# Four matmuls of a modulation burst, placed side by side in the columns of TensorE

## The chip, the cores and the metric

The kernel runs on one core of one Trainium2 chip. The metric is the device time of one launch in microseconds (us); lower is better. The program computes in float32 throughout: matrices go through TensorE either as float32 (two passes through the array for one matmul in the code, as the instruction counts show) or as pairs of `float32r` tiles, a rounded part and its remainder.

## The reference, cut to what matters

Two layers of a diffusion backbone over 1024 latent tokens and 256 context tokens, width 1024. Each layer is modulated: a vector of 6144 numbers is computed from the condition `c` (for the latent tokens) and another from `c_ctx` (for the context tokens), and its six parts of 1024 serve as shift, scale and gate.

```python
mod_x = (c_act @ p['w_mod'] + p['b_mod'])[:, None, :]
mod_c = (cctx_act @ p['w_mod'] + p['b_mod'])[None, None, :]
sh1x, sc1x, g1x, sh2x, sc2x, g2x = jnp.split(mod_x, 6, axis=-1)
hx = rms_norm(x, p['g_norm1']) * (1.0 + sc1x) + sh1x
# input projection, differential attention | S5 | Fourier mixing, concatenation
x = x + g1x * (mix_x @ p['w_out'])
x = x + g2x * sq_relu_mlp(rms_norm(x, p['g_norm2']) * (1.0 + sc2x) + sh2x, p)
```

The product for the modulation has two rows only (`c` and `c_ctx`), 1024 terms and 6144 columns, so it reads 25 MB of weights for each layer and uses two columns of the TensorE array.

## The kernel before, in words

The first layer's modulation is computed in two places. `mod_first` (L306) makes the first 16 of its 48 blocks of 128 columns while the inputs load. The other 32 blocks, as eight wide blocks of 512 columns, come from `mod_pe` (L394), a generator that runs as a filler inside the first layer's attention. The second layer's modulation is computed on VectorE, in `mod_rest`, and the change leaves it alone.

For a wide block `mod_pe` needs 1024 terms, that is eight matmuls of 128 terms by 512 columns. It takes them in two bursts of four (`hf` 0 and 1). A burst loads four weight tiles of 128x512 (L403, SP's queue; the tiles of two bursts alternate between two sets of buffers, so the load of a burst waits until the burst before the last has let go of its set). Its four matmuls accumulate in one PSUM bank (L417); the stationary operand is two columns of `cf`, the two activated conditions. ScalarE copies the 2x512 result out (L418). After the second burst eight small transposes (L424) bring both halves into 128 partitions, and `mod_apply` (L291) adds the bias (L295), adds the second half (L297, only when it is given four columns) and, for the two scale parts, forms a factor with the norm's weights.

The attention (`attention`, L618) works through 10 tiles of 128 queries (tiles 8 and 9 are context, with 256 keys instead of 1280) and four heads in each: 40 units. A unit computes scores on TensorE (L649; the context part into a bank called `C`, the rest into the pool `s`), maxima on VectorE (L656, L663), exponentials on ScalarE (L665, L666), a combination on VectorE (L677), transposes on TensorE (L691), copies on ScalarE (L692) and the product with the values on TensorE (L695). The part from L677 on runs three units behind the scores. Banks of PSUM: four for the scores of `s`, and four in the pool `b`, which `C`, the transposes, the product with the values, the bursts and the burst's transposes share. After three units of four the loop calls the filler once: first `glu`, then `mod_pe`, so that each wide block takes three calls: first burst, second burst, transposes. The order of the instructions on each engine is worked out by a planner from the priority of the code's order and from modelled durations; each engine then runs its list in order.

The activated conditions are put into `cf` and `cs` at the start of `mod_first` (L309 to L314), early in the kernel.

Of the kernel before, what the change touches and what calls it, by code (L numbers as in the profile page):

```python
# [19 lines left out]
AX = mybir.AxisListType  # L20
# [14 lines left out]
KD = D // 128  # L35
# [32 lines left out]
class Block:  # L68
# [236 lines left out]
    def mod_first(self, l):  # L305
        nc, io = self.nc, self.io  # L306
        W0 = []
        cs = self.c1([128, KD, 4], 'cs', F32R)
        cf = self.cf = self.c1([128, KD, 4], 'cf')  # L309
        ca = self.cact.rearrange('p v k -> p k v')  # L310
        nc.vector.memset(cf, 0.0)
        nc.vector.tensor_copy(cf[:, :, 0:2], ca)
        nc.scalar.copy(cs[:, :, 0:2], ca)
        nc.vector.tensor_tensor(cs[:, :, 2:4], ca, cs[:, :, 0:2], ALU.subtract)  # L314
        for b in range(2):
            ps = [self.pf((4, 512)) for _ in range(2)]
            for k in range(KD):
                raw = self.s5([128, 1024])
                self.fetched = nc.sync.dma_start(raw, io['w_mod'][l, k * 128:(k + 1) * 128, b * 1024:(b + 1) * 1024])
                if b:  # L320
                    W0 += self.in_weights(l, 3, (k,))
                if k % 2 == 0:
                    for j in range(2):
                        nc.tensor.matmul(ps[j], cf[:, k], raw[:, j * 512:j * 512 + 512], start=(k == 0), stop=(k == KD - 1))
                    continue
                w = [self.tl('rt' if b else 'w4', [128, 1024], F32R) for _ in range(2)]
                self.split(raw, *w)
                for j in range(2):
                    for e in range(2):
                        nc.tensor.matmul(ps[j], cs[:, k], w[e][:, j * 512:j * 512 + 512],  # L330
                                         start=(k == 0 and e == 0), stop=(k == KD - 1 and e == 1))
            pt = self.pb((128, 8, 4))
            for j in range(2):
                o = self.tl('qk', (4, 512))
                (nc.scalar.copy, nc.vector.tensor_copy)[j](o, ps[j])
                for i in range(4):
                    nc.tensor.transpose(pt[:, j * 4 + i], o[:, i * 128:i * 128 + 128], self.idn[0:4, 0:4])
            self.mod_apply(l, b * 8, 8, pt)
        return W0
# [54 lines left out]
    def mod_pe(self, l, blocks):  # L394
        nc, io = self.nc, self.io
        bursts = [(b, hf) for b in blocks for hf in range(2)]

        def load(i):
            b, hf = bursts[i]
            ws = []  # L400
            for q in range(4):
                w = self.tl('t2' if i % 2 else ('r2', 'r2', 'r2', 'mw')[q], [128, 512])
                nc.sync.dma_start(w, io['w_mod'][l, (hf * 4 + q) * 128:(hf * 4 + q + 1) * 128, b * 512:b * 512 + 512])  # L403
                ws.append(w)
            return ws

        nxt = load(0)
        yield
        for i, (b, hf) in enumerate(bursts):
            ws = nxt  # L410
            if i + 1 < len(bursts):
                nxt = load(i + 1)
            if hf == 0:
                o = self.bg((2, 2, 512))
            p = self.pb((2, 512))
            for q in range(4):
                nc.tensor.matmul(p, self.cf[:, hf * 4 + q, 0:2], ws[q], start=(q == 0), stop=(q == 3))  # L417
            nc.scalar.copy(o[:, hf], p)  # L418
            yield
            if hf:  # L420
                pt = self.pb((128, 4, 4))
                for j in range(4):
                    for e in range(2):
                        nc.tensor.transpose(pt[:, j, 2 * e:2 * e + 2], o[:, e, j * 128:j * 128 + 128], self.idn[0:2, 0:2])  # L424
                self.mod_apply(l, b * 4, 4, pt)
                yield

    def norm_rb(self, rs, w):
# [1009 lines left out]
```

## Time and profile before

| | |
|---|---|
| time, median of three runs | 3086.21 us (3080.57 to 3086.28) |
| the profiled execution's own time | 3082.04 us |
| span of the profiled execution | 3080.3 us |
| PE busy | 2948.4 us, 96% of the span |
| DVE (VectorE) busy | 1980.6 us, 64% |
| ACT (ScalarE) busy | 1074.5 us, 35% |
| POOL (GpSimd) busy | 590.7 us, 19% |
| attention of the first layer | about 429 to 730 us of the span |
| the sixteen bursts | 473 to 685 us of the span |

PE is TensorE's matmuls and transposes, PEld its weight loads, DVE is VectorE, ACT ScalarE, SPq the queue that issues DMAs. PEclk is the granted clock as a share of full speed. L417 is line 417 of the kernel. A busy PE in this table is not a full PE: matmuls are pipelined and their ends modelled. The chain of waits goes back from the last instruction, at each step to what released it or to the instruction before it on its engine; time on that chain is time that the end depends on.

### The profile page before, as it was taken

The page shows a single profiled execution, that of the slowest core. Times are in us where ns is not written, and L with a number is a line of the kernel's source. Part 1 is how long each engine was busy: PE and PEld are TensorE (multiplying, and loading weights), DVE is VectorE, ACT ScalarE, POOL GpSimd, SP SyncE. Part 2 cuts the span into 40 slices and gives each one's busy share as a digit, 9 for nine tenths or more (in the row PEclk, how much of TensorE's full clock was granted, in tenths as well). Part 3 has the DMA queues.
Part 4 walks back from the last instruction along what each step waited for, and adds up shares of the span by engine and source line. Part 5 has one row for each costly group of instructions (what it writes and reads, how often), then busy time and mean ns, then how long its engine had stood idle before and what let it go on. Part 6 is the DMA issues. An engine that isn't in the chain of part 4 may idle for free.

```text
span 3080.3 us, 41053 instructions
## 1 busy us (share of the span) xinstructions
PE 2948.4 (96%) x15309; PEld 2417.2 (78%) x15309; DVE 1980.6 (64%) x3546; ACT 1074.5 (35%) x2379; POOL 590.7 (19%) x515
## 2 busy tenths in 40 slices
PE   6899989999999999999999999989999999999999
PEld 3567777668888888888888877768889888888887
DVE  7867856666567677676545557959866555455444
ACT  5224436666331121121222243427864222211222
POOL 0644510000100000000266123526631000000000
PEclk9899999999999999999999999999999999999999
DMA  8345473435122232231222044571241111111111
GB/s 301 111 147 163 157 199 102 129 110 159 47 63 88 74 98 76 83 96 42 72 81 82 32 154 142 156 171 51 66 141 42 52 45 55 48 49 42 55 49 65
DMA packets 280852, 299.93 MB, mean 97 GB/s; under 512 B 47159, under 2 KB 191949, under 8 KB 280653
## 3 DMA queue, kind: packets, MB, share of 16 engines
q1 hardware_dynamic: 280652, 297.31, 31.8%
q8 instruction: 120, 1.97, 0.3%
q14 instruction: 80, 0.65, 0.1%
HBM read 229.31 MB, written 67.93 MB: 96 GB/s over the span
## 4 chain that ended last, share of the span: by engine, by line
PE 78%; DVE 8%; DMA 4%; issue 2%; ACT 2%; POOL 1%; SPq 0%; DVEq 0%; POOLq 0%; ACTq 0%
PE b_t L1241 26%; PE b_t L1264 25%; PE b_t L1208 7%; PE b_t L584 4%; PE b_t L695 4%; PE s_t L649 3%; PE b_t L417 2%; PE b_t L611 2%; PE b_t L691 1%; DVE mx L663 1%; DMA qs_t<-QD 1%; DMA s_t<-KD 1%; PE f_t L1124 1%; ACT s_t L665 1%; PE b_t L649 1%
## 5 line engine op out<-in xcount | busy, mean ns | idle before, releaser
L1264 PE MATMUL b_t<-hid_t,w_t 128*128 128x512 f32 (+1 forms) x3840 | 809.2, 370 | 0.0
L1241 PE MATMUL b_t<-s_t,w_t 128*128 128x512 f32 (+1 forms) x3840 | 800.4, 369 | 0.0
L1264 PEld LDWEIGHTS b_t<-hid_t,w_t 128*128 128x128 f32 x3840 | 669.7, 189 | 121.7 <-issue 1.9
L1241 PEld LDWEIGHTS b_t<-s_t,w_t 128*128 128x128 f32 x3840 | 669.1, 189 | 121.2 <-issue 1.1
L1266 DVE SCALAR_TENSOR_TENSOR kv_t<-b_t,mod,kv_t 128x512 f32<-128x512 f32 (+1 forms) x640 | 439.5, 694 | 240.2 <-PE b_t L1264 239.6
L159 ACT CAST w_t<-r_t 128x512 fp32r<-128x512 f32 x336 | 194.8, 619 | 797.3 <-PE b_t L1264 528.9
L584 PE MATMUL b_t<-w_t,s_t 128*128 128x512 f32 (+1 forms) x1392 | 356.7, 411 | 17.9 <-ACT s_t L474 6.0
L160 DVE TENSOR_TENSOR w_t<-r_t,w_t 128x512 fp32r<-128x512 f32 x328 | 230.8, 732 | 208.1 <-ACT w_t L159 207.7
L584 PEld LDWEIGHTS b_t<-w_t,s_t 128*128 128x128 f32 x1392 | 266.7, 198 | 81.7 <-issue 6.8
L133 POOL TENSOR_TENSOR sm<-sm,mhalf 128x8 f32<-128x8 f32 (+3 forms) x66 | 104.0, 1575 | 598.3 <-DVE sm L702 234.0
L1245 DVE TENSOR_TENSOR t_t<-b_t,t_t 128x512 f32<-128x512 f32 x160 | 101.3, 633 | 143.3 <-ACT t_t L1244 143.1
L892 POOL TENSOR_TENSOR bg_t<-pt_t,bw_t 128x256 f32<-128x256 f32 x56 | 42.8, 765 | 740.2 <-DMA bw_t<-BD 662.3
L695 PE MATMUL b_t<-kv_t,kv_t 128*128 128x128 f32 x1312 | 178.8, 281 | 3.0 <-ACT kv_t L692 2.8
L695 PEld LDWEIGHTS b_t<-kv_t,kv_t 128*128 128x128 f32 x1312 | 164.7, 194 | 16.7 <-issue 7.8
L663 DVE TENSOR_REDUCE mx<-s_t 128x1 f32<-128x1024 f32 x128 | 155.0, 1219 | 29.7 <-PE s_t L649 29.1
L1244 ACT ACTIVATE t_t<-b_t 128x512 f32<-128x512 f32 x160 | 88.4, 552 | 216.2 <-PE b_t L1241 216.2
L159 ACT CAST hid_t<-t_t 128x512 fp32r<-128x512 f32 x160 | 92.4, 578 | 204.1 <-DVE t_t L1245 204.0
L665 ACT ACTIVATE s_t<-s_t,mx 128x1024 f32<-128x1024 f32 x128 | 143.7, 1123 | 38.0 <-DVE mx L664 31.1
L160 DVE TENSOR_TENSOR hid_t<-t_t,hid_t 128x512 fp32r<-128x512 f32 x160 | 106.7, 667 | 66.2 <-ACT hid_t L159 66.2
L378 DVE SCALAR_TENSOR_TENSOR ac_t<-bg_t,vc,ac_t 128x512 f32<-128x512 f32 x168 | 118.9, 744 | 33.8 <-DMA bg_t<-in_w_mod_dram 33.6
L649 PE MATMUL s_t<-s_t,qs_t 128*128 128x512 f32 x448 | 128.2, 412 | 8.5 <-ACT s_t L665 5.5
L611 PE MATMUL b_t<-w_t,s_t 128*128 128x512 f32 x480 | 115.8, 395 | 6.6 <-DVE w_t L160 3.4
(332 smaller groups left out, 3550.5 us busy)
## 6 DMA issues: line engine op xcount, KB each, us to landing
r_t<-in_w_ff_dram SPq DMA_DIRECT2D x256, 256.0 KB
bg_t<-in_w_mod_dram SPq DMA_DIRECT2D x96, 256.0 KB
r_t<-in_w_in_dram SPq DMA_DIRECT2D x64, 256.0 KB
qs_t<-QD SPq DMA_DIRECT2D x64, 256.0 KB
XD<-kv_t SPq DMA_DIRECT2D x16, 640.0 KB
KD<-t_t SPq DMA_DIRECT2D x40, 256.0 KB
s_t<-KD SPq DMA_DIRECT2D x32, 320.0 KB
QD<-t_t SPq DMA_DIRECT2D x36, 256.0 KB
```

The lines of the kernel that those rows point to most:

```text
L159: self.nc.scalar.copy(h, raw)
L160: (eng or self.nc.vector).tensor_tensor(l, raw, h, ALU.subtract)
L584: nc.tensor.matmul(p[:, :cols], a[:, ts], W[k][:, b, :cols], start=(n == 0), stop=(n == 23))
L611: nc.tensor.matmul(p, a[:, ts], W[k][:, b], start=(n == 0), stop=(n == 11))
L649: nc.tensor.matmul(dst, QS[e][:, m, h], ST[h][m][:, a:b], start=(e == 0), stop=(e == 1))
L663: nc.vector.tensor_reduce(mx[:, m, 1:2], S, AX.X, ALU.max, negate=True)
L665: nc.scalar.activation(PR[m][:, 0:SEQ], S, AF.Exp, bias=mx[:, m, 0:1], accum_out=sm[:, m, 1:2])
L695: nc.tensor.matmul(o, WT[:, kt * 128:(kt + 1) * 128], V[kt // 5][:, kt % 5, h * 128:(h + 1) * 128], start=(c == 0), stop=(c == len(ks) - 1))
L1208: nc.tensor.matmul(p[:, :w], W[c][a][:, k], b[k][:, s:s + w], start=(n == 0), stop=(n == 23))
L1241: nc.tensor.matmul(p[:, :w], W[a][:, k], b[k][:, s:s + w], start=(q == 0), stop=(q == 23))
L1264: nc.tensor.matmul(p[:, :w], W[a][:, cs], hid[b][:, s:s + w], start=(q == 0), stop=(q == n - 1))
L1266: nc.vector.scalar_tensor_tensor(xs, p[:, :w], self.mod[l][:, 40 + c, g // 2:g // 2 + 1], xs, ALU.mult, ALU.add)
```

## The change

The stationary operand of the bursts becomes `cw`, of 32 columns for each block of 128 terms: the two conditions and 30 columns of zeros. Matmul `q` of a burst writes its 32 rows to partitions `32q` to `32q + 31` of one bank, that is, it uses the array's column group `q`; the four matmuls of the first burst start the four sums and those of the second burst finish them, so the bank is held from the first burst to the second. Then one copy of 128x512 on ScalarE, four transposes of 128x128, and one sum over `q` on VectorE (`reduce_sum`) give the eight numbers for each partition that `mod_apply` takes; it no longer adds a second half. The old `cf` stays in use in `mod_first` alone.

```diff
-        cf = self.cf = self.c1([128, KD, 4], 'cf')
+        cf = self.c1([128, KD, 4], 'cf')
         ...
+        self.cw = self.c1([128, KD, 32], 'cw')
+        nc.gpsimd.memset(self.cw, 0.0)
+        nc.vector.tensor_copy(self.cw[:, :, 0:2], ca)
@@ mod_pe
             if hf == 0:
-                o = self.bg((2, 2, 512))
-            p = self.pb((2, 512))
+                p = self.pb()
             for q in range(4):
-                nc.tensor.matmul(p, self.cf[:, hf * 4 + q, 0:2], ws[q], start=(q == 0), stop=(q == 3))
-            nc.scalar.copy(o[:, hf], p)
+                nc.tensor.matmul(p[q * 32:q * 32 + 32], self.cw[:, hf * 4 + q], ws[q], start=(hf == 0), stop=(hf == 1),
+                                 skip_group_check=True)
             yield
             if hf:
-                pt = self.pb((128, 4, 4))
+                o = self.bg((128, 512))
+                nc.scalar.copy(o, p)
+                pt = self.pb((128, 4, 4, 32))
                 for j in range(4):
-                    for e in range(2):
-                        nc.tensor.transpose(pt[:, j, 2 * e:2 * e + 2], o[:, e, j * 128:j * 128 + 128], self.idn[0:2, 0:2])
-                self.mod_apply(l, b * 4, 4, pt)
+                    nc.tensor.transpose(pt[:, j].rearrange('p q v -> p (q v)'), o[:, j * 128:j * 128 + 128], self.idn)
+                r = self.sm(8).rearrange('p (j v) -> p j v', v=2)
+                nc.vector.reduce_sum(r, pt[:, :, :, 0:2].rearrange('p j q v -> p j v q'), axis=AX.X)
+                self.mod_apply(l, b * 4, 4, r)
                 yield
```

## Rows read from the trace of the kernel before

**Rows 1.** The chain of waits over the whole span, its shares by line.

```profile
by line: PE b_t L1241 25.7%; PE b_t L1264 25.5%; PE b_t L1208 6.5%; PE b_t L584 4.5%; PE b_t L695 3.5%; PE s_t L649 2.8%; issue 1.8%; PE b_t L417 1.6%; PE b_t L611 1.6%; PE b_t L691 1.5%; DVE mx L663 1.2%; DMA qs_t<-QD 0.9%; DMA s_t<-KD 0.9
```

**Rows 2.** The chain in order of time (start us, us, what): bursts, 473 to 685.

```profile
473.38 3.52 PE b_t L417 x8
...
681.77 3.52 PE b_t L417 x8
```

**Rows 3.** The chain in order of time, between the bursts at 544.76 and 564.51.

```profile
549.89 0.69 DVE mx L656
...
559.07 1.55 DVE s_t L677
...
563.89 0.63 PE b_t L709 x4
```

**Rows 4.** L417 alone from 470 to 700: window, us, busy PE PEld, PEclk, DMA, GB/s.

```profile
470.00:700.00 230.00, 57.51 (x128) 9.53 (x128) 1.00 0.38 112
```

**Rows 5.** Matmuls in order of time, 1683 to 1687: L912 (partitions 0-63), L914 (64-127).

```profile
1685.43 0.27 PE L912 MATMUL f_t<-bg_t,bw_t 64*16 64x112 f32 x1
1685.44 0.27 PE L914 MATMUL f_t<-bg_t,bw_t 64*16 64x112 f32 x1
1685.54 0.26 PE L912 MATMUL f_t<-bg_t,bw_t 64*16 64x112 f32 x1
1685.55 0.26 PE L914 MATMUL f_t<-bg_t,bw_t 64*16 64x112 f32 x1
...
```

**Rows 6.** Weight loads of 2 and 16 columns, by line, ns (min/median/max).

```profile
L417 PEld LDWEIGHTS b_t<-t_t,cf x64: 80/85/85, 482.7 to 684.3; 128*2 128x2 f32 x64
L916 PEld LDWEIGHTS f_t<-bw_t x128: 92/93/96, 116.4 to 1686.0; 128*16 128x16 f32 x128
```

**Rows 7.** Stretches: window, us, busy PE PEld DVE ACT POOL, PEclk, DMA, GB/s.

```profile
467.05:691.75 224.70, 215.47 (x1278) 150.70 (x1276) 148.04 (x302) 141.85 (x385) 17.26 (x16) 1.00 0.39 113
2115.00:2245.00 130.00, 126.67 (x938) 116.50 (x938) 111.90 (x223) 108.16 (x289) 86.75 (x55) 1.00 0.21 55
447.87:467.05 19.18, 17.98 (x102) 13.91 (x101) 18.91 (x37) 14.81 (x36) 0.00 (x0) 1.00 0.41 138
...
467.05:498.38 31.33, 31.24 (x195) 23.05 (x194) 23.24 (x46) 21.92 (x58) 2.05 (x2) 1.00 0.35 101
498.38:531.60 33.22, 31.43 (x191) 22.70 (x190) 22.20 (x44) 20.82 (x57) 2.05 (x2) 1.00 0.36 104
...
560.26:592.67 32.41, 30.39 (x177) 21.24 (x176) 25.09 (x48) 22.63 (x60) 2.05 (x2) 1.00 0.34 97
...
652.66:691.75 39.09, 38.69 (x248) 29.41 (x246) 31.12 (x61) 29.03 (x73) 2.49 (x2) 1.00 0.28 79
```

**Rows 8.** The chain in order of time, around the transposes of 490 to 493.

```profile
489.72 1.09 PE b_t L691 x10
...
492.20 0.59 PE b_t L424 x8
```

**Rows 9.** ScalarE in order of time, 479 to 487.

```profile
480.55 1.51 ACT L692 COPY kv_t<-b_t 128x256 f32<-128x256 f32 x3 [1.67 <-PE b_t L691]
...
486.34 0.57 ACT L418 COPY bg_t<-b_t 2x512 f32<-2x512 f32 x1 [1.17 <-PE b_t L417]
```

**Rows 10.** VectorE in order of time: the bias, and the second half.

```profile
492.83 0.17 DVE L295 TENSOR_TENSOR mod<-b_t,bmod 128x8 f32<-128x8 f32 x1 [1.44 <-PE b_t L424]
...
493.03 0.17 DVE L297 TENSOR_TENSOR mod<-b_t,mod 128x8 f32<-128x8 f32 x1
```

**Rows 11.** Groups by line and form: a VectorE reduction, and POOL's first long wait.

```profile
L656 DVE TENSOR_REDUCE mx<-b_t 128x2 f32<-128x512 f32 x38 | 26.0, 686 | 15.2 <-PE b_t L649 14.5
...
L133 POOL TENSOR_TENSOR sm<-sm,mhalf 128x10 f32<-128x10 f32 x1 | 2.2, 2180 | 34.3 <-DVE bg_t L152 34.3
```

**Rows 12.** SP's queue, 460 to 700: us waited in total, times, longest.

```profile
SPq L403 <- PE b_t L417: 105.9, 55, 14.5
```

## The prediction

> **What bounds the kernel now.** I read the shares of the chain of waits first, then that chain in order of time from 470 to 700 us, then the busy time of each engine by stretch. The reader is to see that the end hangs on TensorE almost throughout, and that the bursts, L417, hold 1.6% of the whole chain, some 49 us [rows 1]. In order of time they stand there as pieces of 3.52 us with eight instructions each; the first starts at 473.38, the last at 681.77, and there are fourteen such pieces [rows 2]. The line has 128 matmul records [rows 4]: eight wide blocks, two bursts, four matmuls, two passes each. So there are sixteen bursts of eight passes, 3.52/8 = 0.44 us a pass, and two bursts are not on the chain. One of these two falls between 549.89 and 563.89, where the chain goes through VectorE and ScalarE and TensorE had time to spare [rows 3].
>
> The bursts stand in the first layer's attention, where three engines share the work. From 467.05 to 691.75, in which all the bursts lie, PE is busy 215.5 of 224.7 us, VectorE 148.0, ScalarE 141.9, at a granted clock of 1.00, that is 2.4 GHz [rows 7]. What a shorter burst is worth there depends on whether VectorE can follow. Two stretches without bursts tell: the second layer's attention runs with VectorE busy 111.90 of 130.00 us, 86%, and three units just ahead of the first burst run with VectorE at 18.91 of 19.18 [rows 7]. The clock is full in the second layer's stretch too, so it should not fall when the bursts shrink. Behind the attention the chain is TensorE's L1208, L1241 and L1264, 58% of the whole [rows 1]; time that the attention gives back arrives at the end.
>
> **The burst itself.** The four matmuls of a burst get column groups of their own. No row of this kernel shows two column groups at work together, so the bounds are: nothing overlaps, 3.52 us as now, and everything overlaps, two passes of 0.44, 0.88 us. The nearest rows are those of L912 and L914, which use the upper and the lower 64 rows of the array: a pass of one and a pass of the other start 0.01 us apart, and the next such pair 0.11 and 0.10 us after them [rows 5]. A pass of 112 columns at 0.44 us for 512 is 0.096 us, so a pair costs what one pass costs, plus some 6%. I take the same for four column groups: 2 x 0.44 + 6%, 0.94 us; each burst loses 2.58 us. The stationary operand grows from 2 to 32 columns. A load of 2 takes 85 ns and one of 16 takes 92 [rows 6], so I estimate 100 for 32; four loads before a row of passes are 0.40 us even one after another, and a row of passes takes 0.44, which hides them. If it did not, the burst would be at most 0.4 longer.
>
> One rule of the Trainium skill speaks against this. "TensorE: Matmul & The Clock Gate", in "The mechanism" of its part on row and column tiling, has matmuls start and end strictly in program order. In the code both matmuls of L912, four passes, come before both of L914, and the rows alternate between the two lines [rows 5], so either the order was changed ahead of the engine or the rule does not bind tiles of their own; what it would do here is the first rival. The same page, in "Measured speedup vs the span model", gives 2.38 times for three column groups and 3.07 for four row groups; at 3.07 the burst would be 3.52/3.07 = 1.15 us, an estimate from that page, and the gain 14 x 0.21 = 2.9 us smaller.
>
> **What of it reaches the end.** Fourteen bursts on the chain give 14 x 2.58 = 36.1 us; the two off it give nothing. Then VectorE is late next. If it can be busy no more than 86% of a stretch, as in the second layer, its 23.24 us in 467.05 to 498.38 need 27.0, its 25.09 in 560.26 to 592.67 need 29.1, and its 31.12 in 652.66 to 691.75 need 36.1 [rows 7]. These three stretches can give 4.3, 3.3 and 2.9 us where two bursts each ask for 5.2: 5.1 us are lost, with rounding. The others have room, the fullest of them 22.20 busy of 33.22. If VectorE can run at 98%, as just ahead of the bursts, nothing is lost. I take the loss: 36.1 - 5.1 = 31.0 us.
>
> **The bank held between the bursts.** Before, a bank of the pool `b` was given back when ScalarE had copied a burst's result. Now the first burst's bank is held through the next unit until the second burst's copy, eight times. That unit has three banks for `C`, the values' product and two groups of transposes. The three copies that empty its transposes take 1.51 us on ScalarE, 0.5 each, behind transposes of 1.09 us in all [rows 8, 9]. With one bank fewer the last group of transposes waits for the copy before it: 0.5 us and two hand-overs, some 0.8 us. Where TensorE has value products to do meanwhile, or VectorE is late anyway, it costs nothing; if all three copies come to stand on TensorE's path it is 1.5 us. Bounds 0 and 8 x 1.5 = 12; I take 0.8 in five of the eight units, as three lie in the stretches where VectorE sets the pace: 4.0 us.
>
> **The smaller edits.** Eight transposes of two rows take 0.59 us on the chain and become four of 128 rows; ten such take 1.09, so four take 0.44 [rows 8]: 8 x 0.15 = 1.2 us saved. ScalarE makes eight copies fewer, 0.57 us each [rows 9]; it is not late, so I count nothing; the copy that is left stands ahead of the transposes as before, with other units' work beside it. On VectorE the second addition goes, 0.17 us [rows 10], and a reduction of 32 numbers to 8 for each partition comes; between the 0.17 of a small operation and the 0.69 of the reduction over 512 [rows 10, 11] I take it near the small one, 0.2, so nothing changes. At the upper end it is 8 x 0.5 = 4 us on VectorE, of which a third of the stretches would feel it. The memset of `cw` runs on POOL in the first microseconds; POOL then idles 34.3 us [rows 11]. Its copy is one small operation on VectorE, 0.17. SP waits 105.9 us, 55 times, for L417 to free weight buffers [rows 12]; a shorter burst releases them earlier, so the loads behind them in that queue, the queries' included, come earlier or as now. I count nothing.
>
> **Sum.** 3082.04 (the profiled execution) - 31.0 + 4.0 - 1.2 = 3053.8 us. The median of the runs is 4.2 above that execution and their lowest 1.5 below, so against the median it would be 3058. I put the forecast between, at 3055.
>
> **Rivals.** First, passes keep program order, so only the second pass of one matmul and the first of the next overlap: five rows of passes, 5 x 0.44 + 6% = 2.3 us for a burst, a gain of 1.2 on fourteen, 16.8 us, with no loss at VectorE. Less the full 6.4 for the bank and 1.2 for the transposes: 3082.04 - 11.6 = 3070. For it: the passes before are strictly in order, 0.44 us each. Against it: the alternating rows of L912 and L914. Chance 0.15.
>
> Second, the column groups do not run together, and the change does not do what it says, for instance because four streams of 128 partitions each cannot be fed at once; L912 and L914 together read each partition only once, so they don't speak against this. The burst stays at 3.52 and the sum is +4.0 - 1.2: 3085, no change. Chance 0.12.
>
> Third, slower: the held bank. It costs more than it brings when the price per wide block passes what the block's bursts save. With full overlap that is (31.0 + 1.2)/8 = 4.0 us, beyond any bound above; with no overlap the point is 0.15 us. With nothing overlapped and 1.5 us in each of the eight units it is 3082 + 12 - 1.2 = 3093. For it: `b` is the pool that all of the attention's transposes need. Against: a burst is soon over if it overlaps, and TensorE has other products at hand. Chance 0.11.
>
> **How the numbers follow.** The forecast has 0.62, with its own range 3038 (VectorE and the bank cost nothing: 3082.04 - 36.1 - 1.2 = 3044.7, and some 6 us if the two hidden bursts, 5.2, count after all) to 3066 (the bank at its full 12, the reduction at its upper end). A difference under 0.2%, 6 us, can't be told from none in this kernel. The first rival still counts as faster: 0.77. Same 0.12 is the second, slower 0.11 the third. The range from 3036 to 3088 leaves out the third rival, and little below.
>
> **What would show it.** In the profile after: passes of the new matmul line that start four at a time, and its pieces on the chain near 0.9 us where 3.52 stood; 2.2 would be the first rival, 3.5 the second. VectorE's share from the first burst to the last should rise from 66% to about 75%, and its maxima and L677 should take a larger part of the chain. The time from unit to unit between the two bursts of a block tells the bank's price: TensorE waiting there for L692. A copy `o` that TensorE waits for ahead of the transposes would be a cost that I left out. The prediction is wrong if the burst is short and the end doesn't move: then VectorE's limit or the bank has been priced too low.

## The result and the profile after

| | before | after |
|---|---|---|
| median (range) of the runs, us | 3086.24 (3080.57 to 3089.93) | 3054.81 (3049.63 to 3057.02) |
| profiled execution, us | 3082.04 | 3055.69 |
| after / before | | 0.9899, 95% interval 0.9883 to 0.9915 |

The kernel became some 31 us faster, clear of the 0.2% that can't be told from none; the forecast was 3055. Run again in a later set, beside the kernel before, it took 0.9891 of it (0.9877 to 0.9904).

First the burst. Matmuls of the changed kernel in order of time; L419 is the line of the bursts' matmuls, L700 the product with the values, L654 the scores.

```profile
476.61 0.61 PE L700 MATMUL b_t<-kv_t,kv_t 128*128 128x128 f32 x4
477.15 0.63 PE L419 MATMUL b_t<-r_t,cw 128*32 128x512 f32 x3
477.17 0.62 PE L419 MATMUL b_t<-mw_t,cw 128*32 128x512 f32 x1
477.60 0.61 PE L419 MATMUL b_t<-r_t,cw 128*32 128x512 f32 x3
477.62 0.59 PE L419 MATMUL b_t<-mw_t,cw 128*32 128x512 f32 x1
478.03 1.04 PE L419 MATMUL b_t<-t_t,cw 128*32 128x512 f32 x8
479.00 1.16 PE L700 MATMUL b_t<-kv_t,kv_t 128*128 128x128 f32 x8
```

Four passes start within 0.02 us of each other (three `r_t` and the one from `mw_t` are one burst), the next four 0.45 later. Then the reader is to see what was not foreseen: the second burst, from the `t_t` tiles, follows at 478.03 at once. Both bursts of a block take 477.15 to 479.00, 1.85 us, where the two took 2 x 3.52 before [rows 2]. Seven of the eight blocks look like this one; in the other, at 613.52, the two bursts stand apart, at 1.00 us each.

The new small pieces by line, durations in ns (min/median/max):

```profile
L419 PEld LDWEIGHTS b_t<-t_t,cw x64: 106/110/110, 477.6 to 644.0; 128*32 128x32 f32 x64
L427 PE MATMUL b_t<-idn,bg_t x32: 270/273/273, 490.8 to 659.0; 128*128 128x128 f32 x32
L424 ACT COPY bg_t<-b_t x8: 586/594/616, 479.5 to 645.2; 128x512 f32<-128x512 f32 x8
L429 DVE TENSOR_REDUCE smf<-b_t x8: 178/182/192, 493.0 to 661.6; 128x8 f32<-128x32 f32 x8
```

Stretches of the changed kernel (columns as in [rows 7]): from the unit of the first burst to that of the last, the three units just ahead, and 130 us of the second layer's attention.

```profile
470.89:661.03 190.14, 176.37 (x1249) 145.35 (x1248) 144.79 (x299) 136.25 (x376) 17.95 (x16) 0.98 0.45 133
451.70:470.89 19.19, 18.00 (x103) 13.90 (x101) 18.91 (x37) 14.81 (x36) 0.00 (x0) 1.00 0.41 137
2087.00:2217.00 130.00, 126.66 (x939) 116.50 (x937) 111.88 (x221) 108.38 (x288) 87.32 (x55) 1.00 0.23 57
```

The other two stretches are as before [rows 7]. In the bursts' stretch VectorE does nearly the same work, 144.79 us for 148.04, in less time: 76% of it, where it was 66%. TensorE now has more gaps: 13.8 of 190 us, where it was 9.2 of 225. What it waits for in them (matmuls; us in total, times, longest), first in the changed kernel from 470 to 661, then before from 470 to 700:

```profile
PE s_t L654 <- DMA qs_t<-QD: 2.8, 2, 2.5
PE s_t L654 <- ACT s_t L670: 2.6, 5, 0.6
PE s_t L654 <- ACT jk_t L704: 1.8, 1, 1.8
```

```profile
PE s_t L649 <- DMA qs_t<-QD: 2.4, 2, 1.2
PE b_t L709 <- DVE mx L664: 2.3, 2, 1.2
PE s_t L649 <- ACT s_t L665: 0.6, 3, 0.2
```

The queries' loads hold it nearly as long as before. The scores' wait for exponentials (L670, before L665) has grown from 0.6 to 2.6 us, and the wait behind L704, another operation of ScalarE, is new. No single wait makes up the gaps.

The program by stages, worked out from the starts of the first matmuls of each in one profiled execution of each kernel (us). The first attention runs from the first of its scores to the first matmul of the output projection.

| kernel | up to attention 1 | attention 1 | output projection, MLP | projections of layer 2 | attention 2 | rest |
|---|---|---|---|---|---|---|
| before | 428.9 | 301.3 | 1046.5 | 277.3 | 220.5 | 805.8 |
| changed, first profile | 432.8 | 267.1 | 1046.5 | 280.2 | 221.5 | 805.8 |
| changed, again | 430.7 | 264.3 | 1044.0 | 280.7 | 220.7 | 805.8 |

So the attention gave 34.2 us in the first profile and 37.0 in the second. In the first the stages up to the attention were 3.8 us longer and the later ones 4.0, which brings the span's difference to 26.4; the second, same kernel, is 7.7 shorter in all. Over the twelve kernels profiled here the attention begins between 424.8 and 432.8. That the set-up of the 32-column operand makes it start late isn't borne out: in the second profile it starts 1.8 us later than before, within the 2 us that had been expected of a set-up that costs nothing. Each length of a stage here comes from one profile, and the two of the change differ by 2.8 us in the attention; smaller differences say nothing.

### The profile page after: what moved, and what is told of

Same layout as the page of the kernel before. It is cut to its first block, busy times and chain, and to the rows that moved or that the text cites. A ratio compares the mean times of both kernels' runs of the same rounds, so it can differ in the third digit from the quotient of the medians.

```text
span 3053.9 us, 40975 instructions
## 1 busy us (share of the span) xinstructions
PE 2907.2 (95%) x15277; PEld 2407.3 (79%) x15277; DVE 1977.9 (65%) x3547; ACT 1069.1 (35%) x2371; POOL 592.6 (19%) x516
## 5 line engine op out<-in xcount | busy, mean ns | idle before, releaser
L700 PE MATMUL b_t<-kv_t,kv_t 128*128 128x128 f32 x1312 | 178.0, 280 | 3.9 <-ACT kv_t L697 3.4
L700 PEld LDWEIGHTS b_t<-kv_t,kv_t 128*128 128x128 f32 x1312 | 164.2, 193 | 15.0 <-ACT kv_t L697 9.3
L670 ACT ACTIVATE s_t<-s_t,mx 128x1024 f32<-128x1024 f32 x128 | 143.6, 1122 | 36.6 <-DVE mx L669 29.0
L654 PE MATMUL s_t<-s_t,qs_t 128*128 128x512 f32 x448 | 132.8, 419 | 13.4 <-ACT s_t L670 8.5
```

Source lines behind the costliest of these rows:

```text
L654: nc.tensor.matmul(dst, QS[e][:, m, h], ST[h][m][:, a:b], start=(e == 0), stop=(e == 1))
L670: nc.scalar.activation(PR[m][:, 0:SEQ], S, AF.Exp, bias=mx[:, m, 0:1], accum_out=sm[:, m, 1:2])
L700: nc.tensor.matmul(o, WT[:, kt * 128:(kt + 1) * 128], V[kt // 5][:, kt % 5, h * 128:(h + 1) * 128], start=(c == 0), stop=(c == len(ks) - 1))
```

## The experiments

All were timed in three sets, each beside the kernel before on the same chip, in five rounds. "Attention 1" is the stage's length as in the table above.

| kernel | ratio to before | 95% interval | attention 1, us |
|---|---|---|---|
| the change, again | 0.9891 | 0.9877 to 0.9904 | 264.3 |
| one column group | 1.0006 | 0.9997 to 1.0015 | 301.5 |
| two column groups | 0.9918 | 0.9904 to 0.9931 | 273.3 |
| bank held through a unit | 0.9891 | 0.9877 to 0.9904 | 267.2 |
| group by group | 0.9889 | 0.9876 to 0.9903 | 267.7 |
| no bursts | 0.9861 | 0.9844 to 0.9878 | 258.7 |
| share for POOL | 0.9894 | 0.9880 to 0.9907 | 269.1 |
| share for POOL, without the change | 1.0007 | 0.9999 to 1.0016 | 304.6 |
| short combination | 0.9874 | 0.9856 to 0.9892 | 258.2 |
| short copies | 0.9873 | 0.9857 to 0.9888 | 263.0 |
| more buffers for queries | 0.9892 | 0.9874 to 0.9909 | 266.7 |

**One column group: is it the overlap?**

```diff
-                nc.tensor.matmul(p[q * 32:q * 32 + 32], self.cw[:, hf * 4 + q], ws[q], start=(hf == 0), stop=(hf == 1), ...)
+                nc.tensor.matmul(p, self.cw[:, hf * 4 + q], ws[q], start=(hf + q == 0), stop=(hf == 1 and q == 3))
...
-                r = self.sm(8).rearrange('p (j v) -> p j v', v=2)
-                nc.vector.reduce_sum(r, pt[:, :, :, 0:2].rearrange('p j q v -> p j v q'), axis=AX.X)
-                self.mod_apply(l, b * 4, 4, r)
+                self.mod_apply(l, b * 4, 4, pt[:, :, 0:2])
```

> The change with its overlap alone undone: all eight matmuls of a wide block add up in column group 0, with the 32-column stationary operand, one bank from the first burst to the second, one copy, four transposes. Theory 1 (the gain is the overlap of the column groups): the eight matmuls of a block take 16 passes in a row, about 7.0 us, and the gain is gone, 3082 to 3094 us, ratio 0.999 to 1.003. Theory 2 (the gain is the rest of the edit: two bursts that now follow each other, eight copies fewer, a bank that comes free): most of it stays, 3058 to 3070, ratio 0.991 to 0.995.

Ratio 1.0006: the whole gain is gone. The profile shows the passes one after another again (matmuls in order of time):

```profile
474.73 2.76 PE L419 MATMUL b_t<-r_t,cw 128*32 128x512 f32 x6
477.32 1.02 PE L419 MATMUL b_t<-mw_t,cw 128*32 128x512 f32 x2
478.18 2.74 PE L419 MATMUL b_t<-t_t,cw 128*32 128x512 f32 x6
480.85 1.16 PE L697 MATMUL b_t<-kv_t,kv_t 128*128 128x128 f32 x8
```

Here the bursts of this block follow each other, too, there is one copy in place of two, and the stationary operand has 32 columns; the attention takes 301.5 us, 0.2 from before. So these parts bring nothing and cost nothing that can be measured, and theory 2 falls. (The sum over `q` goes as well, and the copy and the transposes have 32 rows.)

**Two column groups: how much of the overlap arrives?**

```diff
+                g = q % 2
-                nc.tensor.matmul(p[q * 32:q * 32 + 32], ..., start=(hf == 0), stop=(hf == 1), ...)
+                nc.tensor.matmul(p[g * 32:g * 32 + 32], ..., start=(hf == 0 and q < 2), stop=(hf == 1 and q > 1), ...)
```

> Column groups 0 and 1 alone, four matmuls in each of a wide block, transposes of 64 rows. Theory 1 (overlap): a block's 16 passes take 8 rows, 3.5 us in place of 7.0; the change takes 1.9. So some two thirds of the gain, 3062 to 3070, ratio 0.9925 to 0.995. If the gain stops where VectorE sets the pace, less is left between the two and it is nearer to the change: 0.991 to 0.9925. Theory 2 (the rest of the edit): as the change, 0.990.

0.9918, some three quarters of the gain. A block's two bursts, matmuls in order of time:

```profile
472.45 1.48 PE L420 MATMUL b_t<-r_t,cw 128*32 128x512 f32 x5
...
474.19 1.89 PE L420 MATMUL b_t<-t_t,cw 128*32 128x512 f32 x8
476.00 1.16 PE L701 MATMUL b_t<-kv_t,kv_t 128*128 128x128 f32 x8
```

472.45 to 476.00 is 3.55 us, so TensorE gives up 7.04 - 3.55 = 3.49 in each of eight blocks, 27.9 us; the attention got 28.0 shorter. From two groups to four TensorE gives up another 8 x 1.70 = 13.6, and the attention 6.2 or 9.0 (the change's two profiles). Within the 2.8 us of scatter the first two thirds of the relief arrive whole, and of the last third half or two thirds. The expectation left both possible; the second reading (less is left between two and four) is the nearer.

**Bank held through a unit: the term of the prediction.**

```diff
+            with self.tc.issue_after(self.lastv.ins) if hf else nullcontext():   # lastv: last product with the values so far
                 for q in range(4):
                     nc.tensor.matmul(p[q * 32:q * 32 + 32], ...)
```

> The change with one edge more: the second burst may not be issued before the product with the values that stands ahead of it in the code, so the bank is held through a unit, as the prediction had it. The prediction's term for the held bank: slower than the change by 4 us, at most 12, ratio 0.991 to 0.994, and TensorE's transposes wait for ScalarE's copies in the units between the bursts. Rival (a held bank costs nothing here): the change's time, ratio 0.989 to 0.991.

Ratio 0.9891, the change's own. The bursts stand apart, and the bank is held some ten us. Matmuls in order of time:

```profile
472.94 0.63 PE L420 MATMUL b_t<-r_t,cw 128*32 128x512 f32 x3
...
477.23 0.81 PE L697 MATMUL b_t<-idn,s_t 128*128 128x128 f32 x6
478.07 0.71 PE L701 MATMUL b_t<-kv_t,kv_t 128*128 128x128 f32 x4
478.72 0.66 PE L697 MATMUL b_t<-idn,s_t 128*128 128x128 f32 x4
479.22 1.06 PE L701 MATMUL b_t<-kv_t,kv_t 128*128 128x128 f32 x8
...
482.38 1.06 PE L420 MATMUL b_t<-t_t,cw 128*32 128x512 f32 x8
```

The unit's ten transposes are split, six and four, and the last four come 0.68 us after the six have ended. Such a split is what the prediction priced; that the held bank makes it isn't shown, since the changed kernel has units split in the same way, at 521.45 for one. But products with the values stand in the gap, and the attention (267.2) is as long as in the change's own profiles (264.3, 267.1). The waits that the prediction named are hardly there: over the whole program the transposes waited for ScalarE's copies once, for 0.2 us. Twelve us are excluded; less than the intervals' 4 us can't be told.

**Group by group: do passes keep the list's order?**

```diff
-            for q in range(4):
-                nc.tensor.matmul(p[q * 32:q * 32 + 32], self.cw[:, hf * 4 + q], ws[q], ...)
+            for q in range(4) if hf else ():
+                for e in range(2):
+                    nc.tensor.matmul(p[q * 32:q * 32 + 32], self.cw[:, e * 4 + q], (wp, ws)[e][q], ...)
+            wp = ws
```

> The change with the eight matmuls of a wide block issued at the second burst, the two of one column group next to each other: groups 0 0 1 1 2 2 3 3. If passes keep their order in the list, each group runs its four passes alone and only the joints overlap: 13 rows of passes, 5.7 us a block, and most of the gain goes: ratio 0.996 to 0.999. If each column group works through its own passes while the others do theirs: 4 rows, about 1.9 us a block as in the change, ratio 0.989 to 0.991.

0.9889, as the change. The list now has the matmul from an `r_t` tile, then the one from a `t_t` tile of the same group, then the next group; on the engine (matmuls in order of time):

```profile
481.93 0.64 PE L420 MATMUL b_t<-r_t,cw 128*32 128x512 f32 x3
481.97 0.62 PE L420 MATMUL b_t<-mw_t,cw 128*32 128x512 f32 x1
482.38 0.62 PE L420 MATMUL b_t<-r_t,cw 128*32 128x512 f32 x3
482.42 0.59 PE L420 MATMUL b_t<-mw_t,cw 128*32 128x512 f32 x1
482.81 1.06 PE L420 MATMUL b_t<-t_t,cw 128*32 128x512 f32 x8
```

All first passes, then all second passes, then the `t_t` tiles: four rows, 1.9 us. The fourth group starts 0.04 us after the first, where it was 0.02 in the change, whose list has only half as many instructions between the two. This fits groups that each take their own instructions in turn as they arrive. The trace doesn't hold the list itself: its order is read from the code, and the doubled distance between the groups speaks for it. The strict order falls.

**No bursts: how much is left in them?**

```diff
-                nc.tensor.matmul(p[q * 32:q * 32 + 32], ...)      # and the copy, the transposes and the sum
+                r = self.sm(8).rearrange('p (j v) -> p j v', v=2)
+                nc.vector.memset(r, 0.0)
```

> The change without the products of mod_pe: the weight loads stay, the bursts' matmuls, the copy, the transposes and the sum are left out, and zeros take the place of their result. TensorE loses another 8 x (1.9 + 0.44) = 18.7 us. Theory A (VectorE and ScalarE set the pace of much of the attention by now): from two to four column groups TensorE lost 13.3 us and the attention 6.8, so half or less of the 18.7 arrives, 4 to 9 us, 0.986 to 0.9885 of the kernel before. Theory B (TensorE still sets the pace): all of it, 16 to 19 us, 0.9835 to 0.985.

0.9861, attention 258.7. TensorE loses 8 x (1.85 + 0.44) = 18.3 us, and 5.6 or 8.4 of the stage go, a third to a half; the medians of this kernel and of the change in the same set differ by 9.5. From two groups to four the table has 6.2, where the expectation has 6.8. This speaks for theory A. Theory B's 16 to 19 us are far from both figures, though the lower end of the interval, 0.9844, still reaches its range. With no bursts at all the stage would be only that much shorter than it is now.

**Share for POOL, with the change and without.**

```diff
-            k1 = TOK - (512 if l else 0)
+            k1 = TOK - (512 if l or t < 8 else 0)
```

> The change, and in the first layer too the last 512 of 1280 columns of the combination (L682) go to POOL, as in the second layer. VectorE loses some 0.6 us in each of 32 units, 20 us; POOL is nearly idle there. Theory A (VectorE sets the pace): the attention gets 4 to 12 us shorter, 0.985 to 0.9885 of the kernel before. Theory C (ScalarE or the hand-overs set it, or POOL's two operations make the transposes late): no gain or a loss, 0.989 to 0.993.

> The same move to POOL in the kernel before, without the change. Theory A: TensorE sets the pace there, so the 20 us taken from VectorE bring 0 to 4 us, 0.9985 to 1.0005. If it brings as much here as with the change (4 to 12 us), VectorE was late before the change as well, and the gain of the change says nothing of a new limit.

With the change 0.9894, no gain; without it 1.0007, just above theory A's range. The operations on POOL (ns, min/median/max):

```profile
L684 POOL TENSOR_SCALAR s_t<-s_t,rr x64: 1563/2314/2812, 453.3 to 2236.4; 128x512 f32<-128x512 f32 x64
L685 POOL TENSOR_TENSOR s_t<-s_t,s_t x64: 1263/1279/1980, 455.2 to 2238.8; 128x512 f32<-128x512 f32 x64
```

One after the other they take 3.6 us where VectorE saves 0.5. But the transposes hardly wait for them: in the first attention the profile puts one wait of TensorE down to L685, 1.1 us. What went wrong stands on VectorE itself. Its lines in the attention (busy us, mean ns; idle before), first of the change, then of the change with the move to POOL:

```profile
L682 DVE SCALAR_TENSOR_TENSOR s_t<-s_t,rr,s_t 128x1280 f32<-128x1280 f32 x32 | 49.5, 1547 | 0.6
L669 DVE TENSOR_TENSOR mx<-mx 128x1 f32<-128x1 f32 x64 | 9.2, 151 | 0.1
```

```profile
L682 DVE SCALAR_TENSOR_TENSOR s_t<-s_t,rr,s_t 128x768 f32<-128x768 f32 x32 | 33.8, 1055 | 0.4
L669 DVE TENSOR_TENSOR mx<-mx 128x1 f32<-128x1 f32 x64 | 21.1, 336 | 0.2
```

The combination saves 15.7 us, and three lines of small operations (L669, L673, L680) take 16.4 more. Of their 136 operations 23 took over 0.4 us, all of them while POOL was at work. So VectorE got no time back: it was busy 226.6 us in this attention, 223.6 in the change's. The same holds without the change (221.2 against 223.6, with L664 at 18.4 us for 11.6). Neither run is a test of what VectorE's time is worth, and whether VectorE was late before the change stays open; the next run tells for the changed kernel.

**Short combination and short copies: which engine's time counts?**

```diff
# short combination
-            k1 = TOK - (512 if l else 0)
+            k1 = TOK - (512 if l or t < 8 else 0)
-            if k1 < TOK:
+            if l and k1 < TOK:
# short copies
-                nc.scalar.copy(WT[:, s:s + w], p[:, :w])
+                c1 = w if l else w // 2
+                nc.scalar.copy(WT[:, s:s + c1], p[:, :c1])
```

> The change, and the first layer's combination (L682) covers 768 of 1280 columns; the other 512 are left out, on POOL as well. VectorE loses some 0.6 us in each of 32 units, nothing else changes and nothing comes later. In the move to POOL the same relief brought nothing, which leaves open whether VectorE has no part in the pace or POOL made the transposes late. Theory A (VectorE sets the pace): 4 to 12 us off the change, 0.985 to 0.9885 of the kernel before. Theory D (no single engine; the round of scores, maxima, exponentials and back to the scores' two buffers): under 3 us, 0.988 to 0.991.

> The change, and the first layer's copies of transposed weights (L697) take half of the columns; the other half is left out and stays zero. ScalarE loses some 0.5 us in each of 32 units and each copy comes earlier. Theory S (ScalarE sets the pace): 4 to 12 us off the change, 0.985 to 0.9885. Theory D: under 3 us, 0.988 to 0.991.

The short combination takes 0.9874 in all, and its attention 258.2 us, 6 or 9 less than the change. L682 takes 33.0 us there in place of 49.5, so 16.5 us taken from VectorE give six to nine; from 470 us on the clock was 1.00 in this attention, and part of the difference may be the half clock that the change's profiles show (last section). The combination also ends 0.5 us earlier for the transposes that follow it, which this run can't tell from VectorE's busy time. With that said, VectorE's time is part of the pace, and theory D's "under 3" fails by the stage. The short copies take 0.9873 in all, inside theory S's range, but their attention is 263.0, only 1 or 4 us below the change, with the clock at 0.98 from 470 to 655; the rest of their gain lies in stages that the edit does not touch. By the stage ScalarE counts for little; by the ratio alone it can't be told apart from VectorE, and this is left open.

**More buffers for queries.** `qs=6` in place of `qs=4`.

> The change with six buffers for the queries' tiles in place of four, so that a tile's load can be issued a tile earlier. In the chain of the kernel with two column groups the queries' loads and their issue hold some 9 us of the first attention. Theory Q (their landing is now late): 3 to 9 us off the change, 0.986 to 0.9885 of the kernel before. Theory D: under 2 us, 0.9885 to 0.991.

0.9892, attention 266.7: nothing. Theory Q falls.

No version tried here that computes the whole result beats the change.

## Why the prediction was right

The forecast held, and it was right for its main reason: the four column groups run together, and TensorE's time on the chain was the attention's time. By its own steps:

- The burst. Predicted 0.94 us, from L912 and L914. Measured 1.85 for two, 0.93 each. The weight load, estimated at 100 ns, takes 106 to 110, and four of them are hidden.
- The first rival, strict order, falls by the rows of the change and by the kernel with neighbours of one group; a burst is now 3.8 times as fast as the 3.52 before. The rule of the Trainium skill that spoke for this rival ("TensorE: Matmul & The Clock Gate", "The mechanism") does not hold across column groups here: the rows above disagree with it, with the list in the order of the code. The estimate from the same page's "Measured speedup vs the span model" was 1.15 us a burst; the trace has 0.93.
- The second rival, no overlap, falls; the kernel with one column group shows what it would have been, 1.0006.
- "Fourteen bursts on the chain, the two off it give nothing." This is doubtful. With two groups TensorE gave up 27.9 us over all sixteen bursts and the stage got 28.0, where fourteen would give 24.4 and the cheaper transposes 1.6. What is left, 2 us, is less than the difference of the two profiles of the change, so it isn't shown that the two count.
- "Then VectorE is late next." Right in kind: the change lets TensorE give up 8 x 5.19 = 41.5 us on the bursts and 1.2 on the transposes, 42.7 in all, and 34.2 or 37.0 arrive. The loss is 5.7 to 8.5, where the prediction lost 10.3 (5.1 to VectorE's share and 5.2 for the two bursts). The short combination speaks for a part of VectorE's in it; that it is all of it is not shown. Over the whole stretch VectorE is busy 76%, well under the 86% that the prediction took as its limit, and another part is the clock.
- "The clock is full ... so it should not fall." It fell: in both profiles of the change parts of the attention ran at half clock (last section). The prediction put nothing down for this.
- The held bank, +4.0: mis-sized; it is not measurable. The step failed twice. The planner issues the second burst right behind the first, since it needs no bank of its own any more, so the bank is held for 2 us and a copy and not through a unit (that this is the reason is argued from the order, not tested). And where it is held through a unit, the time is the same; the rows there show TensorE with other products to do. With this the third rival falls as well.
- The transposes, the copy and the reduction cost what was said: 0.18 us for the reduction, 0.59 for the copy.

Of the signs that the prediction named, the passes that start four at a time and VectorE's share (75% foretold, 76% measured) are there, and TensorE did not wait for the copy `o`. The chain of the changed kernel has no piece between 470 and 661, so what it would say of the burst, the maxima and L677 can't be read. In the kernel with two groups it can: from 470 to 690 the maxima over the scores hold 8.1% of it, where they held 4.8% before, and the combination 2.3%, where it was 2.1%.

Two of the deductions were too large, by 2 to 5 and by 4 us, so the sum's gain of 28.2 lies below what the attention gained, 34 to 37. Against this the stages outside the attention were longer than before, by 7.8 and 2.8 us in the two profiles. Against the median the sum is 3058, and 3055 was put between that and 3053.8. That the median came out within 0.2 us of it is luck; that the gain is some 30 us is not: in the two sets the medians differ by 31.4 and by 34.2 us.

## What to carry to other kernels

Float32 matmuls with few output columns, whose results may be added up later, can share the array: four on four column groups took the time of one here, at the price of one transposing and adding step, and the list needs no special order for it. What such a relief is worth in a stage with several busy engines is told by giving it in steps: here the first 28 us arrived whole, and of the next 13.6 half or two thirds. A long hold of a buffer need not cost anything: a bank held for ten us cost nothing that could be measured here. Ask what the waiting engine has at hand meanwhile. And work moved off a busy engine is a relief only if that engine's other operations keep their length; look at its busy time after the move.

## What the runs showed of the hardware

Four streams of 128 partitions each, from four different tiles, fed the four column groups at no cost in time: a row of four passes of 512 columns starts every 0.43 us, as a single pass did.

Small operations of VectorE, 0.15 us each on L669 of the change, took up to 1.25 us while POOL worked on 128x512 tiles. (In the three lines counted above, none over 0.4 us stood outside POOL's operations.)

In the first profile of the change TensorE waited 1.82 us, until 521.15, before a matmul of the scores, and the granted clock then fell. Stretches of the changed kernel:

```profile
520.00:521.00 1.00, 0.00 (x0) 0.00 (x0) 0.90 (x5) 0.21 (x2) 0.00 (x0) 1.00 1.06 299
521.00:522.00 1.00, 0.85 (x6) 0.81 (x7) 1.00 (x1) 0.13 (x1) 0.00 (x0) 0.94 0.60 154
522.00:523.00 1.00, 1.00 (x6) 0.82 (x5) 0.24 (x1) 1.00 (x5) 0.00 (x0) 0.50 0.03 10
523.00:524.00 1.00, 1.00 (x5) 0.92 (x4) 0.73 (x3) 0.81 (x4) 0.00 (x0) 0.50 0.00 0
524.00:525.00 1.00, 1.00 (x4) 0.79 (x3) 0.14 (x1) 0.41 (x1) 0.00 (x0) 0.50 0.06 16
```

From 522 to 525 it ran at 0.50, that is 1.2 GHz, and the unit there took 7.5 us. In the second profile of the same kernel TensorE was idle at the same place for about as long, 1.73 us, the clock stayed at 1.00, and the unit took 6.2. There it fell later, after a wait of 1.43 us that ended at 547.52 (stretches of the second profile):

```profile
546.00:548.00 2.00, 0.57 (x6) 0.51 (x6) 1.77 (x6) 0.53 (x3) 0.00 (x0) 1.00 0.94 269
550.00:552.00 2.00, 2.00 (x6) 1.18 (x5) 1.01 (x1) 1.84 (x5) 1.92 (x2) 0.50 0.03 13
```

In the first profile it fell once more, to 0.57 on average from 624 to 628. Before the change every stretch of the bursts had 1.00 [rows 7], the longest wait of TensorE in them was 1.2 us, and the prediction took the clock to stay. With the shorter bursts TensorE waits longer, and in both profiles some of the attention ran at half clock, at a cost of 1.3 us in the one unit where the two can be compared. This is part of why the same stage took 267.1 us once and 264.3 the other time. The kernel with two groups and the short combination had 1.00 throughout from 470 us on, so some of what the step from two groups to four lost went here.
